# Two products for three on 256 tokens: high and low parts side by side, halves added by VectorE

## The chip, the cores and the metric

The kernel runs on one core of a Trainium2 chip. The metric is the device time of one execution in microseconds. The engines go by the names of the profile: PE is TensorE (PEld its weight loads), DVE VectorE, ACT ScalarE, POOL GpSimd, SP the engine that issues most DMAs.

## The reference

In fp32, a batch of one: a latent of 256 tokens and a context of 256 tokens, width 1024. Two layers mix both by three gated branches (differential attention, spatial gating, neighbourhood attention) and end in a mixture of 32 experts; in the second layer the context only serves as keys and values. Then one more block on the 256 tokens: gated linear attention (GLA), a short convolution and dilated attention as branches, and a gated FFN of 2816. Cut to the lines whose products the change touches:

```
p = xn @ w_in[l]                                   # layers: all projections; l = 1: 256 latent tokens
yb = einsum('bnie,ied->bnid', stack([y_a, y_b, y_c]), w_branch[l])
g = sigmoid(p_gate.reshape(..., 3, D_MODEL));  h = h + gt1 * (sum(g * yb, axis=2) @ w_out[l])
...
z = h @ w_in[l]                                    # the last block, 256 tokens
y_sc = sc_b * causal_dwconv(sc_c * sc_x, sc_conv_w[l])
gates = sigmoid(h @ w_gate[l] + b_gate[l]);  proj = einsum('bsgc,gcd->bsgd', br, w_branch[l])
...
gt = causal_dwconv(h @ w_ff_gate[l], ff_conv_w[l]) + ff_conv_b[l]
y = (gelu(gt, approximate=True) * (h @ w_ff_up[l])) @ w_ff_down[l]
```

## The kernel before

An fp32 product is made of three products in a 32-bit format of less precision: both operands are split into a high part, rounded to that format, and a low part, the rest; the kernel adds high x high, high x low and low x high, and leaves out low x low. Weights come in tiles of 1024x512 by DMA into a ring of three buffers (`wload`, L178). `wpieces` (L184) splits a tile in four pieces of 256 rows: ScalarE copies the high part (`wh`, L148), VectorE subtracts it (`wl`, L149). The activations' parts lie in separate tiles, `xh` and `xl` (for the branches' outputs `yh` and `yl`).

There are two kinds of product. `dense_x` (L193) keeps the tokens stationary, 128 at a time, and streams 512 columns of weights (L222 to L224). `dense_w` (L228) keeps a 128x128 block of weights stationary and streams the tokens: 512 columns in layer 0, 256 in layer 1 and in the last block (block 2 below), except for layer 1's K product of attention C, which takes latent and context together, 512 columns. Its three matmuls per block of weights, a triple below, are L240, L241 and L242:

```
mm(ps[c][:, :n], lhsT=a, rhs=xh[:, j, :n], start=j == 0, stop=False)
mm(ps[c][:, :n], lhsT=a, rhs=xl[:, j, :n], start=False, stop=False)
mm(ps[c][:, :n], lhsT=b, rhs=xh[:, j, :n], start=False, stop=j == J - 1)
```

A tile of 512 output columns fills four accumulators `acc`, one PSUM bank each (there are four; four more banks, `aux`, take everything else). The first two pieces go through all four accumulators, the last two are held back and done accumulator by accumulator, each of which is then evacuated by `evac(c, ps[c])` (L254) while the next is filled. The evacuations on the way: `ev_gate` and `ev_br` of `gate_branch` (L439: ScalarE takes the tanh of a gate product into `G`, VectorE at L451 multiplies the branch product by it into `merged`); in the conv a ScalarE copy to `su`, then `ev_x` (VectorE, L1485 to L1489: product into `su`, a scaling and shifted multiply-adds into `sy`) and `ev_b` (L1493, and the split of the result); in the FFN `ev_gate` (ScalarE L1620, VectorE L1623 with two shifted multiply-adds that read the accumulator, then L1625 and L1627 around a tanh) and `ev_up` (VectorE L1631, and the split into `gh` and `gl`).

The order of the instructions on an engine is not the code's: a scheduler places them by its own costs, so that products fill the gaps of the attention chains. Each engine works its instructions off in that order, and a wait at the head holds up all behind it.

The profile's stages (us): layer 0 up to 640, its experts to 1142; layer 1's mix (mix 1) 1158 to 1469, its experts 1513 to 1975; block 2 from 1988: Q and K of GLA, V, GLA itself 2032 to 2060, the conv's three products and gate product 0 to 2120, projections of the dilated attention to 2224, that attention with gate product 1 to 2290, gate product 2 to 2325, the output product, the FFN's gate and up products 2362 to 2478 and its down product to the end.

Of the kernel before, what the change touches and what calls it, by code (L numbers as in the profile page):

```python
# [85 lines left out]
def bcast(ap, n=128):  # L86
    return bass.AP(tensor=ap.tensor, offset=ap.offset, ap=[[0, n]] + [list(x) for x in ap.ap])


class Builder:  # L90
# [102 lines left out]
    def dense_x(self, src, J, W, xh, xl, tts, evac, hold=0):  # L193

        if self.begun:
            ps, pieces, piece = self.begun.pop()
        else:
            self.tick()
            ps, pieces, piece = self.begin_x(src, J, W, xh, xl)
# [12 lines left out]
    def begin_x(self, src, J, W, xh, xl):  # L212
# [3 lines left out]
        def piece(t, j0, jn, wh, wl):  # L216
            if t not in ps:
                ps[t] = self.acc()
            for jj in range(jn):
                j = j0 + jj  # L220
                a, b = xh[:, j, t * 128:(t + 1) * 128], xl[:, j, t * 128:(t + 1) * 128]
# [6 lines left out]
    def dense_w(self, src, J, W, xh, xl, n, evac, hold=2):  # L228
        mm = self.nc.tensor.matmul
        ps = {}  # L230
# [165 lines left out]
    def mix_norm(self, tp, l, h, mid=None, junk=None):  # L396

        nc = self.nc
        xh = self.p_x.tile([128, 8, 512], FR, name="xh", tag="xh")
        xl = self.p_x.tile([128, 8, 512], FR, name="xl", tag="xl")  # L400
# [11 lines left out]
        for k, (w, j) in enumerate(order):  # L412
            ws = slice(w * 256, w * 256 + 256)
            if k == 4 and mid is not None:
                mid(xh, xl)
# [8 lines left out]
            nc.vector.tensor_copy(xh[:, j:j + 2, ws], x)  # L424
            nc.vector.tensor_tensor(xl[:, j:j + 2, ws], x, xh[:, j:j + 2, ws].bitcast(FT), op=OP.subtract)
        return xh, xl

    def to_yT(self, y, n):

        yh = self.p_y.tile([128, 4, n], FR, name="yh", tag="yh")  # L430
        yl = self.p_y.tile([128, 4, n], FR, name="yl", tag="yl")
        for c in range(4):
# [3 lines left out]
            self.hilo(yh[:, c, :n], yl[:, c, :n], ps[:, :n])  # L436
        return yh, yl

    def gate_branch(self, i, gate_src, br_src, xh, xl, yh, yl, n, merged, bias=None):  # L439
        nc = self.nc  # L440
        for half in range(2):
# [15 lines left out]
            self.dense_w(gate_src[:, half * 512:(half + 1) * 512], 8, 512, xh, xl, n, ev_gate)  # L457
            self.dense_w(br_src[:, half * 512:(half + 1) * 512], 4, 512, yh, yl, n, ev_br)
# [31 lines left out]
    def mix(self, l, xh, xl):  # L490
# [19 lines left out]
        with self.tp("sg", 1, side="right") as sg:  # L510
# [15 lines left out]
            self.dense_x(W(O_ZB), 8, 512, xh, xl, tts, lambda t, ps: gelu2(u2[:, t], ps), hold=2)  # L526
# [14 lines left out]
            self.dense_x(W(O_ZB + 512), 8, 512, xh, xl, tts, ev_v)  # L541
            self.dense_x(W(O_VA), 8, 512, xh, xl, allt, lambda t, ps: nc.scalar.activation(v[:, t], ps, AF.Copy))
# [12 lines left out]
            ybh, ybl = self.to_yT(yb, n)  # L555
# [44 lines left out]
        self.dense_x(W(O_QA), 8, 512, xh, xl, tts, ev_qk(qT))  # L600
        self.dense_x(W(O_KA), 8, 512, xh, xl, allt, ev_qk(kT))
# [44 lines left out]
        self.gate_branch(0, W2(w_in, O_GATE + 1024), I["w_branch"][l, 1], xh, xl, ybh, ybl, n, merged)  # L646

        yh, yl = self.to_yT(ytok, n)
# [4 lines left out]
        self.dense_w(W(O_KC), 8, 512, xh, xl, 512, ev(kT, 512))  # L653
        self.dense_w(W(O_QC), 8, 512, xh, xl, n, ev(qT, n))
        self.dense_x(W(O_VC), 8, 512, xh, xl, allt, lambda t, ps: nc.scalar.activation(v[:, t], ps, AF.Copy))
# [54 lines left out]
        self.gate_branch(1, W2(w_in, O_GATE), I["w_branch"][l, 0], xh, xl, yh, yl, n, merged)  # L710
        yh = self.p_y.tile([128, 4, n], FR, name="yh", tag="yh")
        yl = self.p_y.tile([128, 4, n], FR, name="yl", tag="yl")
        for c in range(4):
            self.hilo(yh[:, c], yl[:, c], yc[:, c, :n])
        self.gate_branch(2, W2(w_in, O_GATE + 2048), I["w_branch"][l, 2], xh, xl, yh, yl, n, merged)
# [500 lines left out]
    def norm_T(self, y, gain, n):  # L1216

        xh = self.p_x.tile([128, 8, n], FR, name="xh", tag="xh")
        xl = self.p_x.tile([128, 8, n], FR, name="xl", tag="xl")
        for j in range(8):  # L1220
# [3 lines left out]
            self.hilo(xh[:, j], xl[:, j], ps[:, :n], scale=gain[:, j:j + 1])  # L1224
        return xh, xl
# [55 lines left out]
    def block2(self, x, y, later):  # L1281
# [8 lines left out]
        xh, xl = self.norm_T(y, vB[:, 0:8], 256)  # L1290
        self.blk_mix(x, y, xh, xl, hbg, later)
# [4 lines left out]
        xh, xl = self.norm_T(y, vB[:, 8:16], 256)  # L1296
        self.blk_ffn(x, y, xh, xl, vB)
# [52 lines left out]
    def blk_mix(self, x, xn, xh, xl, hbg, later):  # L1350
# [24 lines left out]
        self.dense_w(W(0), 8, 512, xh, xl, 256, ev_qk)  # L1375
# [33 lines left out]
        self.dense_x(W(512), 8, 512, xh, xl, range(2), lambda t, ps: nc.scalar.activation(v[:, t], ps, AF.Copy))  # L1409
# [5 lines left out]
        self.dense_x(W(1024), 8, 512, xh, xl, range(2), ev_g)  # L1415
# [62 lines left out]
        yh = self.p_y.tile([128, 4, 256], FR, name="yh", tag="yh")  # L1478
        yl = self.p_y.tile([128, 4, 256], FR, name="yl", tag="yl")
        with self.tp("sc", 1, side="right") as sp:  # L1480
# [11 lines left out]
            def ev_b(c, ps):  # L1492
                nc.vector.tensor_tensor(y[:, c], y[:, c], ps[:, :256], op=OP.mult)  # L1493
                self.hilo(yh[:, c, :256], yl[:, c, :256], y[:, c])

            self.dense_w(W(2064), 8, 512, xh, xl, 256, lambda c, ps: nc.scalar.activation(u[:, c], ps[:, :256], AF.Copy))
            self.dense_w(W(2576), 8, 512, xh, xl, 256, ev_x)
            self.dense_w(W(1552), 8, 512, xh, xl, 256, ev_b)
            if "ysc" in self.debug:
                nc.sync.dma_start(self.debug["ysc"].rearrange("(c p) t -> p c t", p=128), y)  # L1500
        self.gate_branch(0, I["w_gate_2"][0][:, 1024:2048], I["w_branch_2"][0, 1], xh, xl, yh, yl, 256, merged,
                         hbg[:, 8:16])
        yh, yl = self.to_yT(yg, 256)
# [26 lines left out]
        for g in range(3):  # L1530
            self.dense_x(W(3088 + g * 512), 8, 512, xh, xl, range(2), ev_rope(dqT, g))
            self.dense_x(W(4624 + g * 512), 8, 512, xh, xl, range(2), ev_rope(dkT, g))
            self.dense_x(W(6160 + g * 512), 8, 512, xh, xl, range(2),
# [277 lines left out]
```

## Time and profile before

| | |
|---|---|
| median of 3 runs | 2550.33 us (2549.2 to 2555.16) |
| profiled execution | 2552.59 us, its span 2550.6 us |
| mean granted TensorE clock | 0.983 |
| PE busy | 2431.7 us, 95% |
| DVE busy | 1334.0 us, 52% |
| ACT busy | 857.1 us, 34% |

The span runs from the first to the last instruction on the chip. A matmul's time in a row is from its start to the end of its pipeline; back to back, the distance of two starts is what it costs. The same holds in part for VectorE, whose instructions overlap a little. `x2` or `x4` in a row of the timeline are as many instructions in a row, with the time from the first's start to the last's end.

### The profile page before, as it was taken

To read this page: it belongs to the slowest core of one execution; us is meant where nothing else is said; L and a number is where in the kernel's file an instruction comes from. 1 tells how busy PE (TensorE), PEld (TensorE's weight loads), DVE (VectorE), ACT (ScalarE), POOL (GpSimd) and SP (SyncE) were. 2 spreads that over 40 slices of the span, in tenths; PEclk is the share of its full clock that TensorE was granted. 3 is DMA by queue.
4 is the path that set the end of the run, shared out by engine and by line. 5 is a ranking of instruction groups with operands and counts; after the bars stand their busy time and mean duration, and the time that the engine had idled before them with its cause. 6 is when DMAs were issued, how large, how long until landed. Compare 5 with 4: busy or idle time off the path is not lost. (4 is left out here: it accounts for less than half of the span.)

```text
span 2550.6 us, 33738 instructions
## 1 busy us (share of the span) xinstructions
PE 2431.7 (95%) x13632; PEld 1667.2 (65%) x13632; DVE 1334.0 (52%) x2767; ACT 857.1 (34%) x1510; POOL 134.6 (5%) x172
## 2 busy tenths in 40 slices
PE   8999999999899999989999879998988999999998
PEld 5766776678445554437888754443333898898997
DVE  4646535537444444457664553332223686656784
ACT  4334334434211111115444531111111544544663
POOL 1200002003100000001001110000000000000000
PEclk9999999999899999999999989999999999999999
DMA  9743544454899999983233669999999336435452
GB/s 327 219 162 117 174 145 142 147 184 148 345 422 420 421 421 420 421 355 134 99 124 113 193 270 422 421 421 421 421 421 405 134 132 207 149 116 206 156 175 99
DMA packets 177364, 652.48 MB, mean 256 GB/s; under 512 B 15174, under 2 KB 18778, under 8 KB 127666
## 3 DMA queue, kind: packets, MB, share of 16 engines
q1 hardware_dynamic: 169682, 626.97, 63.7%
q0 software_dynamic: 7520, 23.29, 3.1%
q8 instruction: 109, 1.79, 0.3%
q14 instruction: 53, 0.43, 0.0%
HBM read 644.42 MB, written 5.80 MB: 255 GB/s over the span
## 5 line engine op out<-in xcount | busy, mean ns | idle before, releaser
L149 DVE TENSOR_TENSOR wl<-raw,wh 128x1024 fp32r<-128x1024 f32 (+1 forms) x288 | 347.0, 1208 | 294.4 <-ACT wh L148 282.7
L963 PE MATMUL acc<-raw,xg 128*64 128x512 f32 x896 | 400.5, 597 | 25.1 <-DMA raw<-in_moe_w_up 13.3
L148 ACT ACTIVATE wh<-raw 128x1024 fp32r<-128x1024 f32 (+1 forms) x288 | 300.0, 1046 | 314.6 <-PE acc L241 159.0
L965 PE MATMUL acc<-raw,xg 128*64 128x512 f32 x896 | 400.8, 597 | 0.0
L240 PE MATMUL acc<-xh,wh 128*128 128x256 f32 (+1 forms) x1184 | 370.7, 314 | 0.5 <-ACT xh L157 0.5
L241 PE MATMUL acc<-xl,wh 128*128 128x256 f32 (+1 forms) x1184 | 371.0, 314 | 0.0
L242 PE MATMUL acc<-xh,wl 128*128 128x256 f32 (+1 forms) x1184 | 368.9, 312 | 0.1
L963 PEld LDWEIGHTS acc<-raw,xg 128*64 128x64 f32 x896 | 119.5, 137 | 279.1 <-issue 247.9
L240 PEld LDWEIGHTS acc<-xh,wh 128*128 128x128 f32 x1184 | 226.9, 192 | 19.9 <-issue 6.2
L241 PEld LDWEIGHTS acc<-xl,wh 128*128 128x128 f32 x1184 | 227.5, 192 | 14.0 <-issue 4.2
L242 PEld LDWEIGHTS acc<-xh,wl 128*128 128x128 f32 x1184 | 226.8, 192 | 13.9 <-issue 3.4
L222 PE MATMUL acc<-wh,xh 128*128 128x512 f32 x544 | 214.6, 395 | 2.2 <-ACT row L374 2.0
L224 PE MATMUL acc<-wh,xl 128*128 128x512 f32 x544 | 214.3, 395 | 0.0
L223 PE MATMUL acc<-wl,xh 128*128 128x512 f32 x544 | 213.8, 393 | 0.3 <-DVE wl L149 0.3
L987 PE MATMUL acc<-raw,hT 128*64 128x512 f32 x472 | 210.0, 596 | 1.5 <-ACT hT L979 1.5
L989 PE MATMUL acc<-raw,hT 128*64 128x512 f32 x472 | 210.0, 596 | 0.0
L993 DVE TENSOR_TENSOR aux<-aux,g 128x512 f32<-128x512 f32 x126 | 81.9, 694 | 199.1 <-PE aux L1074 199.1
L1099 DVE SCALAR_TENSOR_TENSOR yl<-acc,ws,yh 128x512 fp32r<-128x512 f32 x64 | 48.0, 750 | 221.3 <-ACT yh L1098 221.3
L987 PEld LDWEIGHTS acc<-raw,hT 128*64 128x64 f32 x472 | 61.8, 137 | 121.2 <-issue 114.7
L979 ACT ACTIVATE hT<-aux 128x512 f32<-128x512 f32 x32 | 19.1, 598 | 343.0 <-PE aux L137 343.0
L222 PEld LDWEIGHTS acc<-wh,xh 128*128 128x128 f32 x544 | 102.7, 189 | 29.8 <-issue 5.5
L965 PEld LDWEIGHTS acc<-raw,xg 128*64 128x64 f32 x896 | 119.5, 137 | 0.0
(482 smaller groups left out, 4248.2 us busy)
## 6 DMA issues: line engine op xcount, KB each, us to landing
raw<-in_moe_w_gate SPq DMA_DIRECT2D x59, 2048.0 KB
raw<-in_moe_w_down SPq DMA_DIRECT2D x59, 2048.0 KB
raw<-in_moe_w_up SPq DMA_DIRECT2D x53, 2048.0 KB
raw<-in_w_in SPq DMA_DIRECT2D x42, 2048.0 KB
raw<-in_w_ada SPq DMA_DIRECT2D x22, 2048.0 KB
rawx<-in_moe_w_up SPq DMA_DIRECT2D x11, 2048.0 KB
raw<-in_w_branch SPq DMA_DIRECT2D x18, 1024.0 KB
raw<-in_w_gate SPq DMA_DIRECT2D x6, 2048.0 KB
```

What stands on the lines that cost most here:

```text
L148: self.nc.scalar.activation(hi, src, AF.Copy)
L149: self.nc.vector.tensor_tensor(lo, src, hi.bitcast(FT), op=OP.subtract)
L222: mm(ps[t][:, :W], lhsT=a, rhs=wh[:, jj, :W], start=j == 0, stop=False)
L223: mm(ps[t][:, :W], lhsT=a, rhs=wl[:, jj, :W], start=False, stop=False)
L224: self.last_mm = mm(ps[t][:, :W], lhsT=b, rhs=wh[:, jj, :W], start=False, stop=j == J - 1)
L240: mm(ps[c][:, :n], lhsT=a, rhs=xh[:, j, :n], start=j == 0, stop=False)
L241: mm(ps[c][:, :n], lhsT=a, rhs=xl[:, j, :n], start=False, stop=False)
L242: mm(ps[c][:, :n], lhsT=b, rhs=xh[:, j, :n], start=False, stop=j == J - 1)
L963: mm(ps[0:64], lhsT=xg[:, j, a0:a0 + 64], rhs=wa(j), start=j == 0, stop=j == 7)
L965: mm(ps[64:128], lhsT=xg[:, j, b0:b0 + 64], rhs=wb(j), start=j == 0, stop=j == 7)
L987: mm(py[half][0:64], lhsT=hT[:, c, 0:64], rhs=da(c, half), start=c == 0, stop=c == 3)
L989: mm(py[half][64:128], lhsT=hT[:, c, 64:128], rhs=db(c, half), start=c == 0, stop=c == 3)
```

## The change

A class `Parts` holds high and low part in one tile [128, j, 2, 256], the two of a row of blocks beside each other. Where 256 tokens are the streamed side, `by_both` makes two matmuls of a triple: the weights' high part takes both parts in one product of 512 columns, and the weights' low part the high part in one of 256, added to the left half of the accumulator. The accumulator is then 512 columns wide, and `by_both_sum` has VectorE add its halves into a tile of SBUF (`sum`, three buffers) with one tensor_reduce, from which the evacuations read. In layer 0, with 512 tokens, the parts lie apart and the three matmuls stay. In layer 1 the latent and the context are two tiles of 256; the K product over both is made as two runs of three matmuls of 256 columns into the two halves of the accumulator. `dense_x` reads its stationary blocks out of the new tiles. The tokens' splits write into the new tiles; elsewhere the diff only passes `x` for `xh, xl`.

```diff
+class Parts:
+    def __init__(self, w, *blocks):
+        self.w, self.blocks = w, blocks
+        self.paired = not isinstance(blocks[0], tuple)
+    def part(self, k, j, a, b):
+        i = a // self.w
+        x = self.blocks[i]
+        a, b = a - i * self.w, b - i * self.w
+        return x[:, j, k, a:b] if self.paired else x[k][:, j, a:b]
...
+    def by_both(self, ps, wh, wl, x, j, n, first, last):
+        mm = self.nc.tensor.matmul
+        if x.paired and n == x.w:
+            mm(ps, lhsT=wh, rhs=x.blocks[0][:, j].rearrange("p k t -> p (k t)"), start=first, stop=False)
+            mm(ps[:, :n], lhsT=wl, rhs=x.hi(j, 0, n), start=False, stop=last)
+            return
+        for i in range(0, n, x.w):
+            k = min(x.w, n - i)
+            for w, part, at in ((wh, x.hi, 0), (wh, x.lo, 1), (wl, x.hi, 2)):
+                mm(ps[:, i:i + k], lhsT=w, rhs=part(j, i, i + k), start=first and i == at == 0,
+                   stop=last and at == 2 and i + k == n)
+
+    def by_both_sum(self, ps, x, n):
+        if not (x.paired and n == x.w):
+            return ps
+        s = self.p_whl.tile([128, 256], FT, name="sum", tag="sum", bufs=3)[:ps.shape[0]]
+        self.nc.vector.tensor_reduce(s, ps.rearrange("p (k t) -> p t k", k=2), axis=AX.X, op=OP.add)
+        return s
...
-                mm(ps[c][:, :n], lhsT=a, rhs=xh[:, j, :n], start=j == 0, stop=False)
-                mm(ps[c][:, :n], lhsT=a, rhs=xl[:, j, :n], start=False, stop=False)
-                mm(ps[c][:, :n], lhsT=b, rhs=xh[:, j, :n], start=False, stop=j == J - 1)
+                self.by_both(ps[c], a, b, x, j, n, j == 0, j == J - 1)
...
-            evac(c, ps[c])
+            evac(c, self.by_both_sum(ps[c], x, n))
...
-        xh = self.p_x.tile([128, 8, 512], FR, name="xh", tag="xh")
-        xl = self.p_x.tile([128, 8, 512], FR, name="xl", tag="xl")
+        if l == 0:
+            X = Parts(512, tuple(self.p_x.tile([128, 8, 512], FR, name=f"x{k}", tag=f"x{k}") for k in "hl"))
+        else:
+            X = Parts(256, *(self.p_x.tile([128, 8, 2, 256], FR, name=f"x{w}", tag=f"x{k}") for w, k in enumerate("hl")))
...
         for j in range(8):
-            a, b = self.wal[0][:, j], self.wal[1][:, j]
-            mm(pa[0:16, :256], lhsT=a, rhs=xh[:, j], start=j == 0, stop=False)
-            mm(pa[0:16, :256], lhsT=a, rhs=xl[:, j], start=False, stop=False)
-            mm(pa[0:16, :256], lhsT=b, rhs=xh[:, j], start=False, stop=j == 7)
+            self.by_both(pa[0:16], self.wal[0][:, j], self.wal[1][:, j], X, j, 256, j == 0, j == 7)
+        pa = self.by_both_sum(pa[0:16], X, 256)
```

The scheduler also places instructions anew. Three places of the order follow; a name's number tells buffers apart, and the new program has other line numbers (the matmuls of a triple are L252 and L253, the reduce L265, the weight split L169).

TensorE at the start of an FFN gate product, before (`wh`, `wl`: the first piece of its weights):

```order
L240 MATMUL acc_19157<-xh_17963,wh_19153 128x256
L241 MATMUL acc_19157<-xl_17964,wh_19153 128x256
L242 MATMUL acc_19157<-xh_17963,wl_19154 128x256
L240 MATMUL acc_19157<-xh_17963,wh_19153 128x256
L241 MATMUL acc_19157<-xl_17964,wh_19153 128x256
L242 MATMUL acc_19157<-xh_17963,wl_19154 128x256
```

and after (`xb` is the tile with both parts; the accumulators are four names in turn):

```order
L252 MATMUL acc_18305<-xb_17541,wh_18301 128x512
L252 MATMUL acc_18310<-xb_17541,wh_18301 128x512
L252 MATMUL acc_18315<-xb_17541,wh_18301 128x512
L253 MATMUL acc_18305<-xb_17541,wl_18302 128x256
L252 MATMUL acc_18305<-xb_17541,wh_18301 128x512
L253 MATMUL acc_18305<-xb_17541,wl_18302 128x256
L253 MATMUL acc_18310<-xb_17541,wl_18302 128x256
L252 MATMUL acc_18310<-xb_17541,wh_18301 128x512
```

The three products of a triple stood together; now products of the high weights for several accumulators stand ahead of the first of the low weights, and a triple is two rows.

VectorE at the conv before, where the evacuations of the second product (`su`, `sy`) begin; `yg` is GLA's output and `wl_15382` the first split of the third product's weights:

```order
L1473 SCALAR_TENSOR_TENSOR yg_15049<-aux_15081,rsy_15097,ggbc_14432 128x128 x4
L149 TENSOR_TENSOR wl_15382<-raw_15379,wh_15381 128x1024
L1474 TENSOR_TENSOR yg_15049<-yg_15049,gs_14720 128x512
L1485 TENSOR_TENSOR su_15121<-su_15121,acc_15251 128x256
L1485 TENSOR_TENSOR su_15121<-su_15121,acc_15258 128x256
L1486 TENSOR_SCALAR sy_15122<-su_15121,vC_93 128x256 x2
```

and after, at the end of those evacuations, with the same split as `wl_15179`:

```order
L265 TENSOR_REDUCE sum_15170<-acc_15087 128x256
L1525 TENSOR_SCALAR sy_14967<-su_14966,vC_93 128x256
L1524 TENSOR_TENSOR su_14966<-su_14966,sum_15170 128x256
L1528 SCALAR_TENSOR_TENSOR sy_14967<-su_14966,vC_93,sy_14967 128x255
L1525 TENSOR_SCALAR sy_14967<-su_14966,vC_93 128x256
L1528 SCALAR_TENSOR_TENSOR sy_14967<-su_14966,vC_93,sy_14967 128x254
L1528 SCALAR_TENSOR_TENSOR sy_14967<-su_14966,vC_93,sy_14967 128x255
L169 TENSOR_TENSOR wl_15179<-raw_15176,wh_15178 128x1024
L1528 SCALAR_TENSOR_TENSOR sy_14967<-su_14966,vC_93,sy_14967 128x254
```

The split stood ahead of the first evacuation and now stands behind the last reduce and six operations that follow it.

VectorE in the FFN before, from the last gate evacuation (`ga`, `fs`) of a pair into the up evacuations (`acc_19026` and on); `wl_19154` and `wl_19186` are the first two splits for the next gate product:

```order
L149 TENSOR_TENSOR wl_19154<-raw_19151,wh_19153 128x1024
L1627 SCALAR_TENSOR_TENSOR ga_18865<-fs_19012,fa_19011 128x256
L1631 TENSOR_TENSOR ga_18865<-ga_18865,acc_19026 128x256
L1631 TENSOR_TENSOR ga_18865<-ga_18865,acc_19033 128x256
L149 TENSOR_TENSOR wl_19186<-raw_19151,wh_19185 128x1024
L158 SCALAR_TENSOR_TENSOR gl_18009<-ga_18865,gh_18008 128x256 x2
L1631 TENSOR_TENSOR ga_18865<-ga_18865,acc_19040 128x256
L1631 TENSOR_TENSOR ga_18865<-ga_18865,acc_19047 128x256
```

and after, at the same place of another pair (splits `wl_18302`, `wl_18326`; `sum_18280` and `sum_18293` are the third and fourth up blocks):

```order
L1669 TENSOR_TENSOR ga_18061<-ga_18061,sum_18267 128x256
L265 TENSOR_REDUCE sum_18280<-acc_18208 128x256
L169 TENSOR_TENSOR wl_18302<-raw_18299,wh_18301 128x1024
L178 SCALAR_TENSOR_TENSOR gl_17586<-ga_18061,gh_17585 128x256
L1669 TENSOR_TENSOR ga_18061<-ga_18061,sum_18280 128x256
L265 TENSOR_REDUCE sum_18293<-acc_18213 128x256
L178 SCALAR_TENSOR_TENSOR gl_17586<-ga_18061,gh_17585 128x256
L1669 TENSOR_TENSOR ga_18061<-ga_18061,sum_18293 128x256
L169 TENSOR_TENSOR wl_18326<-raw_18299,wh_18325 128x1024
```

The first split stood ahead of all four up evacuations and the second between the second and the third; now they stand behind the reduces of the third and of the fourth.

## Rows read from the trace of the kernel before

**Rows 1.** The page's busy times: us (share of the span) x instructions.

```profile
PE 2431.7 (95%) x13632; PEld 1667.2 (65%) x13632; DVE 1334.0 (52%) x2767; ACT 857.1 (34%) x1510; POOL 134.6 (5%) x172
```

**Rows 2.** Busy time by stretch: bounds, length, PE, PEld, DVE, ACT, POOL, clock, DMA.

```profile
1158.00:1469.00 311.00, 302.30 (x1944) 258.94 (x1942) 189.46 (x423) 151.98 (x294) 31.25 (x45) 0.99 0.40 133
2032.00:2060.00 28.00, 26.83 (x247) 24.73 (x246) 25.97 (x55) 8.33 (x23) 0.53 (x1) 1.00 0.18 60
2060.00:2135.00 75.00, 74.97 (x568) 72.01 (x567) 54.19 (x111) 37.27 (x57) 0.00 (x0) 1.00 0.58 197
2290.00:2325.00 35.00, 34.92 (x257) 33.04 (x256) 22.63 (x36) 17.97 (x27) 0.00 (x0) 1.00 0.59 205
2362.60:2478.10 115.50, 115.50 (x963) 115.42 (x962) 92.07 (x165) 70.90 (x125) 0.00 (x0) 1.00 0.46 157
```

**Rows 3.** Timeline of TensorE in the FFN: start, us, engine, line, operation.

```profile
2365.22 0.28 PE L242 MATMUL acc<-xh,wl 128*128 128x256 f32 x1
...
2366.66 0.28 PE L242 MATMUL acc<-xh,wl 128*128 128x256 f32 x1
```

**Rows 4.** Timeline of TensorE, products of 512 columns in block 2.

```profile
2011.78 0.39 PE L222 MATMUL acc<-wh,xh 128*128 128x512 f32 x1
...
2013.37 0.39 PE L223 MATMUL acc<-wl,xh 128*128 128x512 f32 x1
```

**Rows 5.** Groups by form, the 256-column products: count, busy us, mean ns, idle.

```profile
L240 PE MATMUL acc<-xh,wh 128*128 128x256 f32 x896 | 255.8, 287 | 0.5 <-ACT xh L157 0.5
...
L240 PE MATMUL acc<-yh,wh 128*128 128x256 f32 x192 | 54.1, 287 | 1.1 <-ACT yh L154 1.1
```

**Rows 6.** Groups by form on VectorE: a reduce of 512 elements, a rotation of 256.

```profile
L613 DVE TENSOR_REDUCE dax<-aux 128x1 f32<-128x512 f32 x32 | 20.6, 685 | 13.7 <-PE aux L581 13.7
...
L472 DVE TENSOR_TENSOR qrot<-acc,rope 128x256 f32<-128x256 f32 x16 | 6.0, 416 | 0.0
```

**Rows 7.** Timeline of VectorE in attention A: two such reduces back to back.

```profile
1245.64 1.29 DVE L613 TENSOR_REDUCE dax<-aux 128x1 f32<-128x512 f32 x2 [0.77 <-PE aux L581]
```

**Rows 8.** Timeline of VectorE: a subtraction that reads one operand at 32-byte steps.

```profile
1509.42 1.98 DVE L855 TENSOR_TENSOR x2l<-x,x2h 128x1024 fp32r<-128x1024 f32 x1
```

**Rows 9.** Timeline of VectorE in the FFN, one period of a gate and up pair.

```profile
2359.72 1.23 DVE L149 TENSOR_TENSOR wl<-raw,wh 128x1024 fp32r<-128x1024 f32 x1 [3.67 <-ACT wh L148]
...
2369.54 0.42 DVE L1625 SCALAR_TENSOR_TENSOR fs<-fs,fa 128x256 f32<-128x256 f32 x1
2369.88 0.48 DVE L1623 SCALAR_TENSOR_TENSOR fa<-acc,vB,fa 128x255 f32<-128x255 f32 x1
2370.27 1.22 DVE L149 TENSOR_TENSOR wl<-raw,wh 128x1024 fp32r<-128x1024 f32 x1
2371.40 0.42 DVE L1627 SCALAR_TENSOR_TENSOR ga<-fs,fa 128x256 f32<-128x256 f32 x1
...
2382.82 1.23 DVE L149 TENSOR_TENSOR wl<-raw,wh 128x1024 fp32r<-128x1024 f32 x1 [0.53 <-ACT wh L148]
```

**Rows 10.** Timeline of VectorE from GLA's end through the conv's evacuations.

```profile
2062.59 1.22 DVE L149 TENSOR_TENSOR wl<-raw,wh 128x1024 fp32r<-128x1024 f32 x1
...
2068.78 1.22 DVE L149 TENSOR_TENSOR wl<-raw,wh 128x1024 fp32r<-128x1024 f32 x1
...
2070.51 0.75 DVE L1485 TENSOR_TENSOR su<-su,acc 128x256 f32<-128x256 f32 x2
2071.17 0.61 DVE L1486 TENSOR_SCALAR sy<-su,vC 128x256 f32<-128x256 f32 x2
2071.70 1.66 DVE L1489 SCALAR_TENSOR_TENSOR sy<-su,vC,sy 128x255 f32<-128x255 f32 x4
2073.28 0.75 DVE L1485 TENSOR_TENSOR su<-su,acc 128x256 f32<-128x256 f32 x2
```

**Rows 11.** Timeline of TensorE: transposes of GLA's output before a conv product.

```profile
2076.76 0.71 PE L137 MATMUL aux<-glob,yg 128*128 128x128 f32 x5
```

More of the change, by code (lines that the diff above doesn't have):

```diff
@@ L198, in dense_x @@
             self.tick()
-            ps, pieces, piece = self.begin_x(src, J, W, xh, xl)
+            ps, pieces, piece = self.begin_x(src, J, W, x)
         held = []
@@ L423, in mix_norm @@
                                      bias=a[:, w, j + k:j + k + 1], scale=a[:, 2 + w, j + k:j + k + 1])
-            nc.vector.tensor_copy(xh[:, j:j + 2, ws], x)
-            nc.vector.tensor_tensor(xl[:, j:j + 2, ws], x, xh[:, j:j + 2, ws].bitcast(FT), op=OP.subtract)
-        return xh, xl
+            js = slice(j, j + 2)
+            hi, lo = (X.part(k, js, w * 256, w * 256 + 256) for k in range(2))
+            nc.vector.tensor_copy(hi, x)
+            nc.vector.tensor_tensor(lo, x, hi.bitcast(FT), op=OP.subtract)
+        return X
     def to_yT(self, y, n):
-        yh = self.p_y.tile([128, 4, n], FR, name="yh", tag="yh")
-        yl = self.p_y.tile([128, 4, n], FR, name="yl", tag="yl")
+        Y = self.parts_y(n)
         for c in range(4):
@@ L488, in sg_weights, with mix @@
         return ws, hb
-    def mix(self, l, xh, xl):
+    def mix(self, l, X):
         nc, I, tc = self.nc, self.I, self.tc
@@ L1223, in norm_T @@
                 self.T(ps[:, t * 128:(t + 1) * 128], y[:, t, j * 128:(j + 1) * 128])
-            self.hilo(xh[:, j], xl[:, j], ps[:, :n], scale=gain[:, j:j + 1])
-        return xh, xl
+            self.hilo(X.hi(j, 0, n), X.lo(j, 0, n), ps[:, :n], scale=gain[:, j:j + 1])
+        return X
     def prep(self, tp):
@@ L1289, in block2 @@
         vB, hbg = self.vB, self.hbg
-        xh, xl = self.norm_T(y, vB[:, 0:8], 256)
-        self.blk_mix(x, y, xh, xl, hbg, later)
+        X = self.norm_T(y, vB[:, 0:8], 256)
+        self.blk_mix(x, y, X, hbg, later)
         for t in range(2):
@@ L1348, in rope_tables, with blk_mix @@
         return cosT, sinT
-    def blk_mix(self, x, xn, xh, xl, hbg, later):
+    def blk_mix(self, x, xn, X, hbg, later):
         nc, I, tc = self.nc, self.I, self.tc
@@ L1408, in blk_mix @@
         gs = gl.tile([128, 2, 512], FT, name="gs")
-        self.dense_x(W(512), 8, 512, xh, xl, range(2), lambda t, ps: nc.scalar.activation(v[:, t], ps, AF.Copy))
+        self.dense_x(W(512), 8, 512, X, range(2), lambda t, ps: nc.scalar.activation(v[:, t], ps, AF.Copy))
         def ev_g(t, ps):
@@ L1413, in ev_g @@
             nc.vector.scalar_tensor_tensor(gs[:, t], gs[:, t], 1.0, ps, op0=OP.add, op1=OP.mult)
-        self.dense_x(W(1024), 8, 512, xh, xl, range(2), ev_g)
+        self.dense_x(W(1024), 8, 512, X, range(2), ev_g)
         S = gl.tile([128, 2, 4, 128], FT, name="gS")
@@ L1592, in blk_mix @@
             for half in range(2):
-                self.dense_x(I["w_mix_out_2"][0][:, half * 512:half * 512 + 512], 8, 512, mh, ml, range(2),
+                self.dense_x(I["w_mix_out_2"][0][:, half * 512:half * 512 + 512], 8, 512, M, range(2),
                              lambda t, ps: evac(t, half, ps), hold=3 * half)
@@ L1700, in run, with mid @@
                 jobs = []
-                def mid(xh, xl):
-                    ps, pieces, piece = self.begin_x(I["w_in"][0][:, O_ZB:O_ZB + 512], 8, 512, xh, xl)
+                def mid(X):
+                    ps, pieces, piece = self.begin_x(I["w_in"][0][:, O_ZB:O_ZB + 512], 8, 512, X)
                     summed = self.summed
@@ L1741, in run @@
                 self.tail(0, mh, ml, src, hook, next_layer)
-                mh, ml = self.mix(1, *X.pop())
+                mh, ml = self.mix(1, X.pop())
             self.p_res = self.pool(st, "res", side="right")
```

111 lines of the change are left out of this document (57 added, 54 removed).

## The prediction, made before the changed kernel was run

> **What bounds the kernel now.** I read the totals first [rows 1], then the table by stage [rows 2], then the matmuls by form and their starts in the timeline. TensorE is busy 2431.7 of 2550.6 us; VectorE is half idle over the span. The average hides what matters here: the stages that the change touches are full of TensorE work, and some are nearly full on VectorE too. In the FFN's gate and up products TensorE is busy in all of 115.5 us and VectorE in 92.07; at the GLA's end (2032 to 2060) VectorE is busy 25.97 of 28.0 us; in the conv and gate stretch after it 54.19 of 75; in the stretch of gate product 2, 22.63 of 35; in mix 1, 189.46 of 311 [rows 2]. So a product that gets shorter shortens the span only as far as VectorE, which the change loads, keeps up.
>
> **TensorE, what goes.** Before, a triple is three products of 256 columns, each starting 0.120 us after the one before: 12 of them from 2365.22 to 2366.66 [rows 3]. A product of 512 columns takes 1.59 us / 7 = 0.227 us [rows 4]. Both triples stream the same 768 columns; a triple after is one of 512 and one of 256, 0.347 us against 0.360, so it saves 0.0132 us, what one matmul costs beyond its columns. The 256-column triples are 896 + 192 = 1088 [rows 5]: 320 in mix 1 (192 + 32 from the x side, 96 from the y side), 768 in block 2 (32 Q and K, 96 conv, 288 gates and branches, 352 FFN). 1088 x 0.0132 = 14.4 us. Against it, layer 1's K product, whose 512 columns now lie in two tiles, goes from 32 x 3 x 0.227 to 32 x 6 x 0.120: +1.3 us. The eight 16-row triples of the decay projection are worth nothing that counts. Net -13.1 us, and no more than that can be won: no instruction leaves another engine.
>
> **VectorE, what comes.** 160 reduces, 128x512 in PSUM to 128x256 in SBUF, and one of 16 partitions: mix 1 52, block 2's mix 64, FFN 44. No row shows this shape. The nearest reads as many PSUM elements in a row: 0.685 us, and two back to back take 1.29, so the second starts 0.61 after the first [rows 6, 7]. That is my price: 160 x 0.61 = 98 us of VectorE. Below it I see no room: half the input, 256 elements read from PSUM, takes 0.416 [rows 6], and 160 of those would be 67 us. The upper end comes from the access: the reduce takes its pairs from two places 1024 bytes apart. In SBUF a subtraction with one operand at 32-byte steps takes 1.98 us [rows 8], where the same size in a row takes 1.22 [rows 9]: factor 1.62, so 0.61 becomes 0.99 us. Against that stands a rotation that reads PSUM in runs of 16 elements at the price of a contiguous read, 0.416 us [rows 6]; it doesn't jump at each element, so it doesn't settle it. I take 0.61 and keep 0.99 for the range.
>
> The Trainium skill, "Advanced Engine Details and Errata", PSUM Cachelines, speaks against the change: a PSUM line holds two fp32 values, and for best throughput every two consecutive elements should lie side by side, which this reduce never does. By that page's rule it would be the dear one, which is the second rival below; the row of 32-byte steps agrees for SBUF, and no row here shows it for PSUM.
>
> On the other side the evacuations read the sum from SBUF. In the FFN the two shifted multiply-adds of a gate block would start 0.34 instead of 0.39 us apart [rows 9], some 0.06 each, 0.5 us a pair.
>
> **FFN, -3.4.** The period of a gate and up pair is 23.1 us (from the weight split at 2359.72 to that at 2382.82 [rows 9]), of which TensorE uses 192 x 0.120 = 23.04. After, it needs 64 x 0.347 = 22.2. VectorE, 80% busy (92.07 / 115.5 [rows 2]), now works 18.4 us a pair, then 18.4 + 8 x 0.61 - 0.5 = 22.8. So the two engines meet, with VectorE ahead by a hair. Its queue shows where it bites: the next gate's first weight split stands behind the reduce of up block 2, the second behind that of block 3. TensorE, after the last up product at T, has three high products (0.68 us) until it needs the first split. The reduce can start at about T - 1.2 (block 3 takes 4 triples, 1.39 us), 0.61 and 1.13 later [rows 9] the split is there: T + 0.55. It fits with nothing to spare. I take the gain as 352 x 0.0132 = 4.65, less 0.25 us a pair of queueing: 4.65 - 1.3 = 3.4.
>
> **GLA's end and conv, +4.4 of stalls.** Here VectorE is full [rows 2]. Two weight splits are late. (1) The split of the last conv product W(1552), before at 2068.78, ahead of the x evacuation that starts at 2070.51 [rows 10], now stands behind all of it. After the last x product: about 0.2 until the reduce starts, the reduce 0.61, a 256-wide scaling 0.27, a product 0.33, the other scaling 0.27 and three multiply-adds of 0.40 [rows 10], then the split 1.13: 4.0 us. TensorE has four high products (4 x 0.227) and seven transposes of 0.11 [rows 11], 1.7 us: a stall of 2.3. (2) The splits of the x product, before behind one group of GLA scalings (2062.59 [rows 10]), now stand behind four reduces as well: 2.4 us later; with TensorE's cover of a few high products about 2.1 are left.
>
> **The rest.** In mix 1, 52 reduces (32 us) raise VectorE from 61% to 71%; they stand in the attention's softmax chains, whose matmuls the gate products fill. Between 0 and 3 us, I take 1.5. Block 2's gate products 1 and 2 carry 16 reduces each; in the stretch of product 2 VectorE goes from 22.63 to 32.4 of 35 us [rows 2]: 0 to 2, I take 1. A bank of the accumulator is now freed by VectorE where ScalarE did it; three other blocks' first pieces (2 us) stand in front of the bank that is wanted last, which covers 0.61, and not a queue in front: 1.0 us over all stages. Nothing changes in layer 0 or in either MoE; layer 1's weight stream only starts earlier or later with mix 1.
>
> **Sum.** -13.1 + 1.3 (FFN) + 4.4 + 1.5 + 1 + 1 = -3.9 us. The profiled execution took 2552.59 us, so 2548.7 by it; it lies 2.26 above the median of the three runs, 2550.33, inside their spread (2549.2 to 2555.16). From the median: 2546.4 us. About 0.3%, 7.65 us, is what a measurement can tell from no change, so this forecast is "the same". Its own range, by the bounds of the three estimates, is 2542 to 2555.
>
> **Rivals.**
> - *The saving comes through.* VectorE's extra work fits into its idle time in each stage and the scheduler's later splits still find TensorE with something to do. For it: 48% of VectorE's span is idle, and in mix 1 and the FFN the sum leaves just enough. Against it: GLA's 25.97 of 28.0. Then -13.1 + 1 to 4 us: 2538 to 2542. Chance 0.22.
> - *The reduce is dear (about 0.99 us).* From about 0.65 on it decides in the FFN, where VectorE then is the bound: 18.4 - 0.5 + 8 x 0.99 = 25.8 us a pair against 23.1, +2.7 x 5.5 = +15. In the conv and gate stretch 54.19 + 28 x 0.99 = 82 against 75: +7. In gate product 2's, 22.63 + 16 x 0.99 = 38.5 against 35: +3.5. Mix 1 0 to +2. Together about +27: 2577; half way, at 0.8, some +10: 2560. For it: the SBUF row at 32-byte steps. Against it: the rotation's row. Chance 0.23.
> - *Cheap reduce, but queues.* At 0.61 the stalls behind splits come in each pair of the FFN (1 us each, +5.5) and in mix 1's chains (+5), so that they outweigh the saving: -13.1 + 4.4 + 5.5 + 5 + 4 = +6: 2551 to 2560. Chance 0.15, half of it above the measurable bound.
> - *The forecast.* Chance 0.40.
>
> That the change doesn't take effect is no rival: the order of its instructions holds 1088 products of 512 columns and 160 reduces, and the rows of 512 columns exist in layer 0.
>
> **Chances.** Faster by over 0.3%: the first rival, most of it, and a little of the forecast's lower edge, 0.23. Slower by over 0.3%: the second rival, and half of the third, 0.31. The same: 0.46. The range reaches from the lower end of the first rival to just above the second's time: 2538 to 2578.
>
> **What would show it.** Reduce: its mean in the profile, under 0.70 or near 1 us; that number alone tells the forecast from the second rival. FFN: the distance of the first weight splits of two pairs, 22.4 to 22.7 us by me, 22.2 by the first rival, 25 to 26 by the second, where VectorE's busy share would be near 100% and TensorE's idle time would end with VectorE. Conv: idle time of TensorE ended by a weight split, 4 to 5 us between 2060 and 2090, of which before had none that counts [rows 2]. TensorE: the triple at 0.347. If the products of 512 and 256 columns in turn took other pitches than each among its like, or if the sums in mix 1 end the softmax chains, the forecast is wrong.

## The result, and the profile after

| | before | after |
|---|---|---|
| median, 4 runs each | 2550.51 us (2549.2 to 2555.16) | 2567.23 us (2566.32 to 2570.57) |
| profiled execution | 2552.59 us, clock 0.983 | 2566.32 us, clock 0.977 |
| ratio | | 1.0065 [1.005, 1.0079] |

The change made the kernel 16.7 us slower by the medians, 13.7 by the two profiled executions; the forecast was 4 us faster. The page's first line after, against [rows 1]:

```profile
PE 2434.5 (95%) x12632; PEld 1617.4 (63%) x12632; DVE 1422.8 (55%) x2928; ACT 860.3 (34%) x1512; POOL 134.4 (5%) x172
```

TensorE has 1000 instructions fewer and yet is 2.8 us longer busy: what it won was lost in work that ran slower. Where, is seen by following the same instruction through both traces. Each row is a stage and how much its end moved against its begin (after minus before, us; the instructions that bound the stages are in both programs). The forecast's share stands beside it.

| stage | forecast | measured |
|---|---|---|
| layer 0 and its experts | 0 | -2.9 |
| mix 1, to its experts | -1.4 | +4.0 |
| layer 1's experts | 0 | -0.5 |
| GLA, conv, gate product 0, projections (to 2224) | +1.4 | +10.9 |
| dilated attention, gate products 1 and 2 | -1.5 | -1.6 |
| output product and norm | 0 | +5.2 |
| FFN, gate and up | -3.4 | -1.4 |
| FFN, down | 0 | +0.1 |
| all (1 us of the forecast spread over all stages) | -3.9 | +13.9 |

How far such a shift can be trusted differs by stage. In layer 0 and its experts TensorE, VectorE and ScalarE work off the same order of instructions in all eleven changed kernels, and yet the end of this stage lies 4.4 us before to 1.0 us behind that of the kernel before: so much differs between executions with the same order, and why stays open. From GLA to the projections the changed kernel and two of the experiments (the unused products and the early split, below) have the same order too, and the shifts are +10.9, +10.6 and +11.0.

The reduce first. The group by form, the new one and the old one that the price came from (columns as in [rows 6]; the old line L613 is now L657):

```profile
L265 DVE TENSOR_REDUCE sum<-acc 128x256 f32<-128x512 f32 x160 | 108.2, 687 | 19.6 <-PE acc L253 18.7
...
L657 DVE TENSOR_REDUCE dax<-aux 128x1 f32<-128x512 f32 x32 | 20.6, 686 | 13.7 <-PE aux L625 13.7
```

0.687 us against 0.686: taking each element from another place, 1024 bytes away, costs nothing on this read of PSUM, and the rival of the dear reduce falls. The Trainium skill's rule on this ("Advanced Engine Details and Errata", PSUM Cachelines), read as one for VectorE too, does not hold here; the measurement decides.

TensorE's triple next, in the timeline of the FFN, against [rows 3, 4]:

```profile
2399.92 0.40 PE L252 MATMUL acc<-xb,wh 128*128 128x512 f32 x1
2400.16 0.28 PE L253 MATMUL acc<-xb,wl 128*128 128x256 f32 x1
2400.28 0.40 PE L252 MATMUL acc<-xb,wh 128*128 128x512 f32 x1
...
2404.16 0.40 PE L252 MATMUL acc<-xb,wh 128*128 128x512 f32 x1
```

From 2399.92 to 2404.16 lie 12 triples: 0.353 us each, not 0.347. The 256-column product still costs 0.120; the one of 512 costs 0.233 here. The triple saves 0.0067 us, half of what I had: 1088 x 0.0067 - 1.3 = 6 us in all. The trace of before has rows at this price too, 512-column products among their like, in a branch product of layer 0, 9 of them in 2.10 us or 0.233 each:

```profile
228.96 0.39 PE L242 MATMUL acc<-yh,wl 128*128 128x512 f32 x1
...
231.06 0.40 PE L242 MATMUL acc<-yh,wl 128*128 128x512 f32 x1
```

Then the waits of TensorE from 2030 to 2350 (who waited <- for whom: us, times, longest):

```profile
PE acc L243 <- DVE wl L169: 5.4, 2, 4.6
PE acc L253 <- DVE wl L169: 5.3, 2, 2.7
PE acc L252 <- ACT wh L168: 1.0, 1, 1.0
PE aux L1482 <- DVE gK L1475: 0.8, 2, 0.5
PE acc L252 <- DVE sum L265: 0.8, 1, 0.8
```

Three of them are long, each for a weight split of VectorE. The timeline of TensorE at each:

```profile
2054.89 0.58 PE L253 MATMUL acc<-xb,wl 128*128 128x256 f32 x1 [2.67 <-DVE wl L169]
...
2083.12 0.58 PE L253 MATMUL acc<-xb,wl 128*128 128x256 f32 x1 [2.68 <-DVE wl L169]
2083.50 0.63 PE L252 MATMUL acc<-xb,wh 128*128 128x512 f32 x1
2083.93 0.63 PE L253 MATMUL acc<-xb,wl 128*128 128x256 f32 x2
...
2330.93 0.79 PE L243 MATMUL acc<-wl,xb 128*128 128x512 f32 x1 [4.63 <-DVE wl L169]
2331.52 0.63 PE L244 MATMUL acc<-wh,xb 128*128 128x512 f32 x1
2331.95 0.63 PE L242 MATMUL acc<-wh,xb 128*128 128x512 f32 x1
```

Behind the second and third the products stand at half speed: 0.43 us from one 512-column product to the next (2331.52 to 2331.95) where 0.227 is usual. That is the clock. The windows around the three waits and in the FFN (columns as in [rows 2]; the third number from the end is the granted clock):

```profile
2052.00:2064.00 12.00, 9.33 (x52) 8.05 (x51) 7.92 (x20) 3.57 (x19) 0.53 (x1) 0.72 0.47 166
2080.00:2088.00 8.00, 5.32 (x18) 4.44 (x19) 5.92 (x11) 1.06 (x1) 0.00 (x0) 0.58 0.00 0
2328.00:2336.00 8.00, 5.07 (x16) 4.12 (x17) 5.15 (x9) 1.57 (x3) 0.00 (x0) 0.79 0.14 52
2385.00:2475.00 90.00, 89.41 (x505) 76.63 (x503) 88.71 (x158) 55.83 (x94) 0.00 (x0) 1.00 0.48 164
```

A granted clock of 0.72 over 12 us is 2.4 GHz with 1.2 GHz in 6.7 of them. Before, the stretches of [rows 2] around the first two places stood at 1.00, and so did 2325 to 2336, the place of the third. A wait thus costs twice here: itself, and the slow products behind it. From GLA's first product to the first of the dilated attention TensorE idles 9.0 us, where it was 1.2 before: two waits of 2.7, three of 0.7 to 1.0 (the lines above hold them) and small ones. It is busy for 10.9 us of this stage at 1.2 GHz, from 2054.0 to 2060.8 and from 2081.3 to 2088.1 with 0.50 granted; before, it never was. Half of that, 5.5 us, is an estimate of what the clock costs; 7.8 + 5.5, less 1.5 for the 224 shorter triples, is 11.8, and the table has +10.9.

The second wait is the one that the prediction worked out from the order. VectorE's timeline shows its chain, the last reduce, six operations and then the split:

```profile
2079.21 0.68 DVE L265 TENSOR_REDUCE sum<-acc 128x256 f32<-128x512 f32 x1
2079.81 0.34 DVE L1525 TENSOR_SCALAR sy<-su,vC 128x256 f32<-128x256 f32 x1
2080.07 0.42 DVE L1524 TENSOR_TENSOR su<-su,sum 128x256 f32<-128x256 f32 x1
2080.41 0.48 DVE L1528 SCALAR_TENSOR_TENSOR sy<-su,vC,sy 128x255 f32<-128x255 f32 x1
2080.80 0.35 DVE L1525 TENSOR_SCALAR sy<-su,vC 128x256 f32<-128x256 f32 x1
2081.06 0.87 DVE L1528 SCALAR_TENSOR_TENSOR sy<-su,vC,sy 128x254 f32<-128x254 f32 x2
2081.85 1.22 DVE L169 TENSOR_TENSOR wl<-raw,wh 128x1024 fp32r<-128x1024 f32 x1
```

3.9 us from the reduce's start to the split's end, where the prediction had 3.8.

### The profile page after: what moved, and what is told of

Its sections match the earlier page's. It is cut to its first block, busy times and chain, and to the rows that moved or that the text cites. A ratio compares the mean times of both kernels' runs of the same rounds, so it can differ in the third digit from the quotient of the medians.

```text
span 2564.5 us, 31877 instructions
## 1 busy us (share of the span) xinstructions
PE 2434.5 (95%) x12632; PEld 1617.4 (63%) x12632; DVE 1422.8 (55%) x2928; ACT 860.3 (34%) x1512; POOL 134.4 (5%) x172
## 5 line engine op out<-in xcount | busy, mean ns | idle before, releaser
L169 DVE TENSOR_TENSOR wl<-raw,wh 128x1024 fp32r<-128x1024 f32 (+1 forms) x288 | 344.9, 1208 | 233.0 <-ACT wh L168 227.4
L252 PE MATMUL acc<-xb,wh 128*128 128x512 f32 x672 | 240.0, 403 | 1.1 <-DVE sum L265 0.8
L253 PE MATMUL acc<-xb,wl 128*128 128x256 f32 x672 | 187.9, 288 | 6.1 <-DVE wl L169 5.8
L252 PEld LDWEIGHTS acc<-xb,wh 128*128 128x128 f32 x672 | 128.0, 192 | 28.4 <-DVE sum L265 1.5
L253 PEld LDWEIGHTS acc<-xb,wl 128*128 128x128 f32 x672 | 130.0, 194 | 12.0 <-DVE wl L169 9.8
L265 DVE TENSOR_REDUCE sum<-acc 128x256 f32<-128x512 f32 x161 | 108.8, 687 | 19.6 <-PE acc L253 18.7
L1141 ACT ACTIVATE yh<-acc,ws 128x512 fp32r<-128x512 f32 x64 | 44.0, 687 | 208.0 <-PE acc L1032 208.0
L258 PE MATMUL acc<-xl,wh 128*128 128x512 f32 x256 | 102.6, 401 | 0.0
L258 PE MATMUL acc<-xh,wh 128*128 128x512 f32 x256 | 102.4, 400 | 0.0
L258 PE MATMUL acc<-xh,wl 128*128 128x512 f32 x256 | 101.6, 397 | 0.0
L1130 DVE SCALAR_TENSOR_TENSOR hid<-hid,acc 128x512 f32<-128x512 f32 x32 | 22.0, 688 | 141.7 <-PE acc L1008 141.7
```

What stands on the lines that cost most here:

```text
L169: self.nc.vector.tensor_tensor(lo, src, hi.bitcast(FT), op=OP.subtract)
L252: mm(ps, lhsT=wh, rhs=x.blocks[0][:, j].rearrange("p k t -> p (k t)"), start=first, stop=False)
L253: mm(ps[:, :n], lhsT=wl, rhs=x.hi(j, 0, n), start=False, stop=last)
L258: mm(ps[:, i:i + k], lhsT=w, rhs=part(j, i, i + k), start=first and i == at == 0, stop=last and at == 2 and i + k == n)
L265: self.nc.vector.tensor_reduce(s, ps.rearrange("p (k t) -> p t k", k=2), axis=AX.X, op=OP.add)
```

## The experiments

Theory 1, formed on these lines: the loss is made by weight splits that come late in VectorE's queue, at three places, and by the low clock behind each; TensorE itself wins only 6 us. The rivals: the pairing or the new order costs by itself, or the FFN, where VectorE is at its limit (88.71 of 90 us, above), keeps the loss. Shifts of stages are those of the profiled executions, as in the table above.

**Without the sum.**

```diff
-        s = self.p_whl.tile([128, 256], FT, name="sum", tag="sum", bufs=3)[:ps.shape[0]]
-        self.nc.vector.tensor_reduce(s, ps.rearrange("p (k t) -> p t k", k=2), axis=AX.X, op=OP.add)
-        return s
+        return ps[:, :n]
```

> Leaves the sum of the two halves out: the evacuations read the left half of the accumulator, the products of the low token parts in the right half are dropped. All pairing on TensorE stays. Theory 1 (the loss is made by the reduces in VectorE's queue, ahead of weight splits, and by the half clock behind each stall; TensorE itself gains only about 6 us since a 512-column product behind a 256-column one takes 0.233 us): the three stalls of 2.7, 2.7 and 4.6 us and their half clock go, 2540 to 2546 us. Rival (the pairing itself or the new order of the work costs, not the reduces): within 5 us of the changed kernel, 2562 or more.

2548.51 us, ratio 0.9991 [0.9982, 1.0]: 18.7 below the changed kernel, so the reduces, with the order that the scheduler makes for them, are most of what makes it slow. But it is hardly faster than before, 2.5 us above the upper end that I expected. The waits of 2.68 and 4.63 are gone (0.66 is left of the last), the FFN gains 3.3 us and not 1.4. The first wait stays, at the same place and as long, and yet the stage lost nothing there. The wait and the window on it, against the first of the changed kernel above:

```profile
2055.41 0.39 PE L253 MATMUL acc<-xb,wl 128*128 128x256 f32 x1 [2.67 <-DVE wl L169]
```

```profile
2052.00:2064.00 12.00, 9.33 (x71) 8.26 (x68) 10.49 (x31) 5.38 (x23) 0.53 (x1) 1.00 0.43 149
```

TensorE is busy as long, 9.33 us, and does 71 matmuls in place of 52: here the clock did not fall. So this wait is not the reduces' doing: in the changed kernel too it ends at 2054.89, and the conv's first reduce starts at 2063.66. It comes with the pairing of the conv's products and their new order (without that pairing it is gone, below). What it cost the changed kernel was the clock: from GLA's first product to the last of its output it took 29.5 us there, 26.8 here and 26.8 before. Why the clock held in this execution stays open.

**ScalarE takes half of the sum.**

```diff
-        self.nc.vector.tensor_reduce(s, ps.rearrange("p (k t) -> p t k", k=2), axis=AX.X, op=OP.add)
+        self.nc.scalar.activation(s, ps[:, n:], AF.Copy)
+        self.nc.vector.tensor_tensor(s, ps[:, :n], s, op=OP.add)
```

> The sum in another way: ScalarE copies the right half to SBUF, VectorE adds the left half to it (one operation of 256, 0.34 us apart, for the reduce's 0.60: 160 x 0.26 = 42 us less on VectorE, 66 us more on ScalarE). Theory 1 (late splits behind VectorE's reduces): each split behind four reduces comes about 1 us earlier, the three stalls shrink, some fall under what lowers the clock: 2553 to 2561 us. Rival A (it is the wait for a second engine, not VectorE's load): as the changed kernel or slower, 2567 to 2575, since the chain gets longer. Rival B (neither): 2567.

2557.18 us, 1.0026 [1.0015, 1.0036]: 10 us back. The wait at W(1552) shrinks from 2.68 to 1.09, that before the output product from 4.63 to 1.62, and behind these two the clock stays at 1.00; the output stage goes from +5.2 to -0.2. It is VectorE's load that makes these two splits late, not the wait for another engine: rival A falls. The first wait, 2.68 us, and its low clock (0.72 from 2052 to 2064) are left, and the stage of the conv still loses 7.6 us.

**Products of one size in a row.**

```diff
+                for jj in range(jn):
+                    j = j0 + jj
+                    mm(ps[c], lhsT=wh[:, jj, c * 128:(c + 1) * 128],
+                       rhs=x.blocks[0][:, j].rearrange("p k t -> p (k t)"), start=j == 0, stop=False)
+                for jj in range(jn):
+                    j = j0 + jj
+                    mm(ps[c][:, :n], lhsT=wl[:, jj, c * 128:(c + 1) * 128], rhs=x.hi(j, 0, n), start=False,
+                       stop=j == J - 1)
```

> Within a piece, the two 512-column products of an accumulator stand together, then the two 256-column ones; all else as changed. Theory 1 (a 512-column product costs 0.233 behind a 256-column one and 0.227 behind another, so the alternation takes half of the gain): half of the alternations go, the triple falls from 0.353 to 0.350 us, 1088 x 0.0032 = 3.5 us: 2563 to 2565. Rival (0.233 belongs to the form, moving data with two parts of one tile, whatever stands before): triple stays at 0.353, 2566 to 2568.

The triple falls more than expected, to 4.18 us / 12 = 0.348 (`x2` is two products):

```profile
2394.72 0.63 PE L280 MATMUL acc<-xb,wh 128*128 128x512 f32 x2
2395.19 0.39 PE L284 MATMUL acc<-xb,wl 128*128 128x256 f32 x2
...
2398.90 0.63 PE L280 MATMUL acc<-xb,wh 128*128 128x512 f32 x2
```

So the order counts, but not as Theory 1 had it. Two products of 512 columns still take 0.47 us (2394.72 to 2395.19), 0.233 each over the six groups, the one behind its like no less than the one behind 256 columns. It is the 256-column product that fell, from 0.120 to 0.116. In so far the rival is right: the 0.233 did not go with the alternation, and why 512 columns cost 0.227 in one product and 0.233 in another stays open. The kernel gained 11 us, 2556.41, 1.0017 [1.0008, 1.0026], where the triple gives 1088 x 0.005 = 5.4: the scheduler's order changed with it. In the conv, two waits of 1.6 and 1.7 us are left of 2.67 and 2.68 and the stage loses 2.9 instead of 10.9 us; before the output product TensorE waits as long as ever, 4.80 us (+6.1). Triple and order are mixed in the total; only the pitch is measured by this run.

**Pairing in the FFN alone** (a switch `self.pair`, set in `blk_ffn`; elsewhere the three matmuls).

> Pairing and reduces in the FFN alone; everywhere else three products of 256 columns and no sum, from the new tiles. Theory 1: the FFN gains 352 x 0.0066 = 2.3 us less some 0.5 us of late splits a pair, so 0 to 2.3 us, and the three stalls before it go: 2546 to 2551. Rival (the FFN, with VectorE near 100%, is where the loss is): 2553 to 2560.

2554.32 us, 1.0012 [1.0003, 1.0022], 3 us above my range's end; the profiled execution, at 2551.18, was the fastest of 11. The FFN itself moved by -0.4 us, since the first gate block starts 2 us later, and the conv and the output product by -0.1 and 0: no loss in the FFN, and hardly a gain. Mix 1 lost 4.9 us in this execution, and has no pairing at all in this kernel (below). What puts the median 2.4 us above the kernel before of the same rounds, this one trace doesn't show.

**Warm through the wait** (12 unused matmuls ahead of the output product).

```diff
+            self.keep_warm(self.last_mm, 12)
             for half in range(2):
```

> The changed kernel with 12 unused matmuls on TensorE (195 columns, fp32, about 4 us at full clock) between gate product 2 and the output product of block 2, where TensorE waited 4.63 us for a weight split and then ran at half clock. Theory 1 (a stall costs twice, itself and the half clock behind it): the wait stays in place, filled, the products behind it start 0.23 us apart and not 0.43, and from gate 2's last tanh to the norm before the FFN 1.5 to 2.5 us go: 2565 us. Rival (the low clock belongs to this place whatever TensorE did before): no change there, 2567, or 4 us more if the split is not late for the reason that I think.

The timeline of TensorE, with the unused products as L164 (each of these fp32 products is two instructions):

```profile
2328.49 4.12 PE L164 MATMUL acc<-glob 128*128 128x195 f32 x24
2332.31 0.77 PE L242 MATMUL acc<-wh,xb 128*128 128x512 f32 x2
2333.77 0.50 PE L243 MATMUL acc<-wl,xb 128*128 128x512 f32 x1 [0.69 <-DVE wl L169]
2334.10 0.39 PE L244 MATMUL acc<-wh,xb 128*128 128x512 f32 x1
2334.33 0.40 PE L242 MATMUL acc<-wh,xb 128*128 128x512 f32 x1
```

The split comes as late as before, and the products behind it stand 0.23 us apart. The stage loses 3.9 instead of 5.2 us: 1.4 us of it had been the clock, the rest the wait. The total, 2567.23, 1.0055 [1.0038, 1.0071], doesn't show 1.4 us.

**An early split.**

```diff
+            if half and hook:
+                hook()
             self.dense_w(br_src[:, half * 512:(half + 1) * 512], 4, 512, y, n, ev_br)
```

`hook` is given by gate product 2 alone: it loads the output product's weights and splits their first piece.

> The changed kernel with the first weight piece of the output product split ahead of gate product 2's last branch product; all else as changed. Theory 1 (the 4.63 us are the split's place in VectorE's queue behind four reduces and their evacuations): the first split is ready in time, the second comes about 2.4 us after TensorE has used up the first: the stall goes from 4.6 to at most 2.5 us, with less half clock: 3 to 5 us less, 2562 to 2564. Rival (TensorE waits there for the merged branches, not for the split): 2566 to 2568.

The wait falls from 4.63 to 1.95 us, the clock stays at 1.00 behind it, and the stage loses 1.7 instead of 5.2 us. 2563.75, 1.0042 [1.0028, 1.0056]: 3.5 below the changed kernel, as expected, though the two intervals still overlap. The stage shows it: it was the split's place in the queue.

**No pairing in the conv** (the switch off around its three products).

> The changed kernel without pairing in the conv's three products (three matmuls of 256 columns, no reduces there); all else as changed. Theory 1 (GLA's end is where VectorE is full, and 12 reduces and the new order there make two stalls of 2.7 us with half clock): of the 10.9 us that this stretch lost 8 to 10 come back: 2557 to 2559. Rival (the loss there is spread, or comes from gate product 0's reduces): 2563 or more.

2555.13 us, 1.0012 [1.0002, 1.0021]: 12 us back. All that TensorE waits from 2030 to 2140 is this:

```profile
PE aux L1483 <- DVE gK L1476: 1.0, 2, 0.6
PE acc L244 <- DVE wl L170: 0.4, 1, 0.4
```

The stage goes from +10.9 to 0.0. 96 of 1088 triples, worth 0.6 us, carried the greatest loss.

**The three mends together** (products of one size in a row, early split, no pairing in the conv).

> Together: within a piece the two 512-column products in a row and then the two 256-column ones, the early split of the output product, and no pairing in the conv. Theory 1: from the reordered kernel's 2556.4, 3 us in the conv and 4 to 6 in the output product: 2547 to 2550, level with the kernel before. Rival (the parts are not additive, since the scheduler places the stalls elsewhere): 2553 or more.

2552.59 us, 1.0001 [0.9991, 1.001]: level with before, 2.6 us above my range. The conv stands at -0.3, the output product still waits 2.94 us (+3.4).

**Pairing where it pays** (products of one size in a row; no pairing in the conv and in gate product 2).

> Pairing where the runs so far show no late split behind it: not in the conv, not in gate product 2; with the two 512-column products of a piece in a row. Theory 1: against the kernel with all three mends (2552.6), the output product's wait of 2.9 us and its half clock go, 3.3 us, and 1.2 us of gate product 2's gain with them: 2549 to 2552, 0 to 3 us below the kernel before. Rival (the FFN's reduces or mix 1's keep the rest): 2553 to 2556.

2548.80 us, 0.999 [0.9981, 0.9999], 0.2 below my range. The output product's stage is at 0.0.

**And ScalarE's half in the FFN.**

> As the selective kernel, and in the FFN ScalarE copies the right half and VectorE adds the left one, instead of the reduce. Theory 1 (the FFN stands at VectorE's limit: 89 of 90 us busy, late splits cost about 1 us a pair): VectorE gets 8 x 0.26 = 2.1 us a pair free, the FFN's period falls from about 22.6 to 22.3 us, the FFN gains 4 us and not 2.6: 1 to 2.5 us below the selective kernel. Rival (the longer chain through ScalarE costs it back): level with it or up to 3 us slower.

2546.19 us, 0.9984 [0.9976, 0.9993]: 4 us, 0.16%, faster than before, the best version found. Its interval overlaps with that of the selective kernel, but up to the FFN the two have the same order of instructions, so the step is read in the FFN: gate and up gain 3.7 us, and the down product keeps that; with the reduce, gate and up gain 3.0, and the down product loses 1.4 of it again, waiting 0.30 and 0.50 us for weight splits. The difference is 2.1 us. The windows of the selective kernel and of this one in the same 90 us:

```profile
2385.00:2475.00 90.00, 88.90 (x509) 77.08 (x508) 88.92 (x163) 57.09 (x99) 0.00 (x0) 1.00 0.48 165
```

```profile
2385.00:2475.00 90.00, 90.00 (x513) 77.76 (x512) 83.31 (x166) 67.46 (x135) 0.00 (x0) 1.00 0.51 172
```

VectorE falls from 88.92 to 83.31 us, and TensorE has no more gaps. In the FFN the reduce had taken a good part of the gain.

## Why the prediction was wrong, point by point

The step that failed is the price of late weight splits. The term for GLA's end and the conv counted two waits, 4.4 us, and nothing for what stands behind a wait; the stage showed 7.8 us of waits and about 5.5 us of products at 1.2 GHz. The term for the gate products put 1 us where the split for the output product cost 5.2. And TensorE's gain was 6 us, not 13.1. With the conv's pairing off, 12 us come back, with an early split 3.5; that is the evidence for the first two.

- **The bound by stage: right.** VectorE is what decides, and where it was called nearly full it did: GLA's end and conv, the stretch of gate product 2, the FFN at 88.71 of 90.
- **The reduce's price: right**, 0.60 us from start to start and 0.687 busy, at the lower of the two ends. The loss lies between the two prices of the dear reduce's rival, +10 and +27 us, but its cause was wrong.
- **TensorE's gain: half.** The step took the pitch of 512 columns, 0.227, from one product, and the paired form runs at 0.233 in either order; the rows of layer 0 at that price were in the trace of before. 13.1 us should have been 6. (The rows give 0.0129 us a triple, not 0.0132; that is 0.4 us in all.)
- **The conv: the place right, the size not.** The wait behind W(1552) was put at 2.3 us and is 2.68. The other one was put at the second product and behind four reduces; it came at the first, 2.67 us, ahead of any reduce of the conv; that its size fits is luck. The stage was to lose 1.4 us net and lost 10.9. What failed most is that a wait was counted once: behind both the clock stood at 1.2 GHz. Three waits of 0.7 to 1.0 us were not in the sum at all. The trace of before could have told: behind a wait of 4.80 us at 1987.7 the granted clock is 0.81 from 1988 to 2008. I had not asked what a new wait does to the clock.
- **The output product: missed, 5.2 us.** I worked out gate product 2's stretch as 32.4 of 35 us for VectorE and put 1 us on gate products 1 and 2 together. The sum of a stretch doesn't show what its last instruction keeps waiting: two reduces, four operations of their evacuations and five token splits still stood ahead of the split when TensorE had done its last branch product.
- **The FFN: -3.4 forecast, -1.4 measured**, 2.3 us of gain by the measured triple, less 1 us at its begin; of the small waits, forecast at 0.25 us a pair, the gate and up products show 0.7 us in all.
- **Mix 1: +4.0, not settled.** Its stage moved by +4.0 in the changed kernel, by +3.6, -0.6 and -0.5 in three others in which TensorE, VectorE and ScalarE have the same order of instructions there, and by +4.9 in the one without pairing there. So most of the +4.0 can be one execution's. The windows at the end of attention C in the kernels without conv pairing, with FFN pairing alone, and as changed:

```profile
1428.00:1448.00 20.00, 14.09 (x81) 10.23 (x82) 9.64 (x34) 8.22 (x25) 6.48 (x10) 0.83 0.60 183
```

```profile
1428.00:1448.00 20.00, 14.81 (x72) 11.05 (x73) 8.76 (x32) 8.45 (x26) 4.50 (x7) 0.58 0.62 183
```

```profile
1428.00:1448.00 20.00, 14.39 (x65) 10.31 (x66) 7.06 (x28) 6.99 (x21) 5.64 (x9) 0.53 0.53 148
```

The granted clock differs, 0.83 against 0.58 and 0.53; before the change it was 0.83. TensorE waits there for the softmax chain in all of them, before the change too (3.73 us at 1433). So this stage swings by 4 to 5 us from execution to execution, and the clock with it; that the pairing has a part in it was not shown.
- The third rival, cheap reduce and queues, had the right mechanism, with +6 us and a chance of 0.15; it lacked the clock and the output product.

## What to carry to other kernels

Before work is put on an engine that is "half idle", look for the instructions of that engine for which the bound engine waits next, and count what will stand ahead of each in its queue at the end of a stage: the busy share of a stretch doesn't show it. Where TensorE is the bound, price a new wait with the slow clock behind it, here up to about the wait's own length again (an estimated 5.5 us behind two waits of 2.7). A faster form of the inner product pays only where the engine that has to clean up after it has room: here in the FFN, with the cleaning shared by ScalarE, and in two of the gate products.

## What the runs showed of the hardware

- A 512-column product costs 0.227 us in some products and 0.233 in others; in the paired form it is 0.233 behind 256 and behind 512 columns alike. With two and two in a row the 256-column product falls from 0.120 to 0.116, and the pair of 512 and 256 from 0.353 to 0.348 us.
- VectorE's reduce over PSUM costs the same whether it reads 512 elements in a row (0.686 us) or jumps 1024 bytes at each (0.687).
- Behind waits of TensorE of 2.67, 2.68 and 4.63 us in the changed kernel the clock fell to 1.2 GHz for some microseconds. The wait's length alone doesn't tell when: behind 1.09, 1.62 and 1.95 us in other kernels it held, behind 1.57 in the reordered one it held and behind 1.74 there it fell (0.74 granted from 2076 to 2080), and behind 2.67 it held in the kernel without the sum.
- With the same order of instructions on TensorE, VectorE and ScalarE, layer 0 and its experts ended up to 5.4 us apart in eleven executions.
